# Finishing the softmax sums of a hybrid block's attention on GpSimd

## The chip, the cores and the metric

The kernel runs on one core of a Trainium2 chip. The metric is the device time of one execution in microseconds (us), as the median of several runs. The core has five engines, each with a queue of its own that it works off in order: TensorE (PE, with its weight loads PEld), VectorE (DVE), ScalarE (ACT), GpSimd (POOL) and SyncE (SP), which issues DMAs. ScalarE and GpSimd issue DMAs too, from the same queues as their arithmetic.

## The reference

One layer of a decoder block over 2048 tokens of 1024 features in float32: a combined projection feeds sliding-window attention (8 query heads over 2 key heads of 64, window 128, a learned sink for each head) and a chunkwise mLSTM; both are merged, and a gated feed-forward part follows. The change lies in the softmax of the attention:

```python
m = jnp.maximum(jnp.max(s, axis=-1, keepdims=True), sink)
p = jnp.exp(s - m)
p = p / (jnp.sum(p, axis=-1, keepdims=True) + jnp.exp(sink - m))
o = jnp.einsum('bnhgqk,bnkhd->bnqhgd', p, vb)
```

The sink takes part in the maximum and in the sum, but has no value vector.

## The kernel before

The 2048 tokens go through in four blocks of 512 rows, two blocks to a superblock. The first superblock's attention falls between about 110 and 300 us, the second's between about 760 and 960 us. Float32 products are made of three matmuls of high and low parts; the big projections (`acc` tiles, PSUM) are a long stream of 512-wide matmuls that keeps TensorE going. All matmuls are issued by one helper (L212) and all transposes by another (L217), so the trace shows those two lines; what an operation is, its tiles tell.

The attention is written as `attention(n, ...)`, L957 to L1038, for 128 queries, n = 0 to 15. Because of the window, 128 queries see 128 own keys and the 128 before; the two triangles fit together into one 128x128 tile for each head. The eight heads are treated as two halves of four heads (`jj`):

- Scores: matmuls `mix<-at` (L981 by way of the helper), copied out of PSUM by ScalarE (L985) and merged with the previous keys by VectorE's predicated copy (L987) into `sc[jj]`, a `tm` tile of 128x512.
- Maxima on VectorE (L993 to L996), with the sinks; `es` is the exponent of the sinks (L997, ScalarE).
- For each half four exponentials on ScalarE (L1002), which also add up each row into `sums`.
- For each half: VectorE adds the sinks' share to the sums (L1003), VectorE takes the reciprocal (L1004), GpSimd multiplies the half's 128x512 by it (L1005).
- Some time later (a yield of `L_SOFT` = 8000 on the estimated clock): four transposes a half on TensorE (`mix<-ident,tm`), a copy by ScalarE (L1014) and a masked copy by VectorE (L1018), and the weighted sum of the values (`mix<-tm,at`, L1026).
- The result goes out in a high and a low part: L1030 on ScalarE, L1035 on VectorE, with DMAs from ScalarE's queue (L1032, L1037). The operands of a later n are loaded from the same queue (L954).

GpSimd's queue holds, beside the multiply, the stores of q, k and v (L806, L833, L851, L853), a few operations of the mLSTM (L1098, L1100, and at L1149 a power with exponent -0.5 on 128x4), the power of the norms (L492) and memsets.

Where this work stands among the other is decided twice. Python generators (`spawn`, `tick`) place the attention's pieces in the stream of projection matmuls by a running estimate of TensorE's time; then, after the first block's opening, a scheduler orders each engine's queue by its own simulated timeline (L2237). So an edit in one engine's operations can move the place of operations on all engines. The memsets of constants are at L187 and L188.

Of the kernel before, what the change touches and what calls it, by code (L numbers as in the profile page):

```python
# [10 lines left out]
F32 = mybir.dt.float32  # L11
# [4 lines left out]
ALU = mybir.AluOpType  # L16
# [3 lines left out]
P = 128  # L20
# [53 lines left out]
def decoder_block(ctx: ExitStack, tc: tile.TileContext, a: dict, out: bass.AP, dbg=None):  # L74
# [19 lines left out]
    V, A, T, Q = (InOrder(e) for e in (nc.vector, nc.scalar, nc.tensor, nc.sync))  # L94
    G = nc.gpsimd
# [4 lines left out]
    const = ctx.enter_context(tc.tile_pool(name="const", bufs=1))  # L100
# [13 lines left out]
    def nm(s):  # L114
        uid[0] += 1
        return f"{s}{uid[0]}"
# [68 lines left out]
    halves = const.tile([P, 8], F32, name="halves")  # L185
    nhalf, half_pi = halves[:, 0:4], halves[:, 4:5]
    G.memset(nhalf, -0.5)  # L187
    G.memset(half_pi, PI / 2)  # L188
    inv_freq = const.tile([P, HD // 2], F32, name="inv_freq")
    for i in range(HD // 2):  # L190
# [578 lines left out]
    def superblock(sb):  # L769
# [187 lines left out]
        def attention(n, a_, ahead):  # L957
# [11 lines left out]
            sums = small.tile([P, HQ], F32, tag="sums", name=nm("sums"))  # L969
            es = small.tile([P, HQ], F32, tag="es", name=nm("es"))  # L970
# [27 lines left out]
            for jj in range(2):  # L998
                hs = slice(4 * jj, 4 * jj + 4)
                for i in range(4):  # L1000
                    c = 4 * jj + i
                    A.activation(sc[jj][:, i, :], sc[jj][:, i, :], AF.Exp, bias=nm_[:, c:c + 1], accum_out=sums[:, c:c + 1])  # L1002
                V.tensor_tensor(sums[:, hs], sums[:, hs], es[:, hs], op=ALU.add)  # L1003
                V.reciprocal(sums[:, hs], sums[:, hs])  # L1004
                G.tensor_tensor(sc[jj], sc[jj], sums[:, hs].unsqueeze(2).to_broadcast([P, GQ, P]), op=ALU.mult)  # L1005
            yield L_SOFT
            ps_ = []
# [34 lines left out]
        def attention_stream(u):  # L1042
            a_ = None
            for i in range(u, 2 * NT, 2):
                n = b0 * NT + i
                if a_ is None:
                    while i >= ready[0]:
                        yield 1000.0
                    a_ = load_at(n, nc.sync)
                    yield L_LOAD  # L1050
                    a_ = yield from attention(n, a_, lambda: i + 2 < ready[0])
                else:
                    yield L_LOAD - 1500.0
                    a_ = yield from attention(n, a_, lambda: i + 2 < ready[0])
                done_att[0] += 1
                yield 500.0
# [1179 lines left out]
def build(nc, aps, out):  # L2236
    with tile.TileContext(nc, schedule_with_timeline_sim=True) as tc, ExitStack() as ctx:  # L2237
        decoder_block(ctx, tc, aps, out[0])
# [16 lines left out]
```

## Time and profile before

| quantity | value |
|---|---|
| median of 3 runs | 2663.15 us (2661.76 to 2663.3) |
| the profiled execution | 2668.66 us |
| its span in the profile | 2667.0 us |
| mean granted clock of TensorE | 0.994 |
| exponentials L1002, ScalarE, 128 of them | 0.392 us each |
| GpSimd's multiply L1005, 32 of them | 34.6 us in all |
| GpSimd's stores of q, L806, 32 of them | 17.8 us in all |

The profile is of one execution. Its engines' busy times count arithmetic; a wait is put down to the operation that came last before the waiting instruction began. The granted clock says at what share of its full speed TensorE was allowed to run in a stretch. A row of the timeline gives start and duration in us, the engine, the line, the operation and its tiles, and in brackets the idle time of the engine before it with its releaser; rows that follow each other alike are merged, and the ends of matmuls are modelled.

### The profile page before, as it was taken

What the parts mean: (1) busy time and instruction counts of PE and PEld (TensorE: products, weight loads), DVE (VectorE), ACT (ScalarE), POOL (GpSimd) and SP (SyncE); (2) the same over time, 40 slices, a digit from 0 to 9 for tenths busy, and PEclk for the clock granted to TensorE, in tenths of its full rate; (3) what the DMA queues carried; (4) which work ended last, traced back from release to release, by engine and by line L of the source; (5) the groups of instructions that cost most, each with busy time, mean ns of one, the idle gap of its engine ahead of it and who ended that gap; (6) DMA issues with size and microseconds to landing.
All of it is one profiled execution on the core that took longest, in us unless ns stands there. A gap on an engine that the chain in (4) does not pass through costs nothing.

```text
span 2667.0 us, 36229 instructions
## 1 busy us (share of the span) xinstructions
PE 2615.5 (98%) x12546; PEld 2145.8 (80%) x12546; DVE 1937.2 (73%) x3758; ACT 1281.9 (48%) x2531; POOL 300.3 (11%) x473
## 2 busy tenths in 40 slices
PE   8999999999989999999999999999999999999998
PEld 6877788888876788888878888888778888888876
DVE  5878887768676988875777777775776767676466
ACT  6656544545654654454643433345554333333444
POOL 0320001101132000210001111110000011001000
PEclk9899999999999999999999999999999999999999
DMA  7785465887787545597765554446675323234556
GB/s 270 255 303 164 135 196 183 291 301 253 262 313 244 166 135 181 183 296 268 220 238 193 184 169 153 163 139 228 213 242 173 111 99 116 90 111 139 199 196 220
DMA packets 327032, 532.97 MB, mean 200 GB/s; under 512 B 23136, under 2 KB 197724, under 8 KB 320064
## 3 DMA queue, kind: packets, MB, share of 16 engines
q1 hardware_dynamic: 287752, 448.45, 50.4%
q0 software_dynamic: 20880, 66.41, 6.6%
q10 hardware_dynamic: 18216, 15.79, 1.9%
q8 instruction: 99, 1.62, 0.2%
q14 instruction: 85, 0.70, 0.1%
HBM read 367.61 MB, written 154.57 MB: 196 GB/s over the span
## 4 chain that ended last, share of the span: by engine, by line
PE 88%; DVE 4%; DMA 3%; ACT 2%; issue 1%; POOL 0%; ACTq 0%; SPq 0%; DVEq 0%; POOLq 0%
PE acc L212 62%; PE mix L212 22%; PE mix L217 2%; PE acc L90 1%; DVE hl L1745 1%; PE mix L90 1%; DMA raw<-as_d 1%; ACT hl L1744 1%; DMA big<-big 0%; DMA raw<-ws_d 0%; DMA raw<-in_w_in_dram 0%; ACT tm L1002 0%; DMA at_d<-tx 0%; DMA raw<-in_w_ffn_down_dram 0%; ACT big L575 0%
## 5 line engine op out<-in xcount | busy, mean ns | idle before, releaser
L212 PE MATMUL acc<-big,hl 128*128 128x512 f32 x3936 | 936.4, 393 | 7.0 <-ACT tx L870 5.4
L212 PEld LDWEIGHTS acc<-big,hl 128*128 128x128 f32 x3936 | 733.8, 188 | 166.4 <-ACT tx L870 5.9
L1744 ACT CAST hl<-raw 128x512 fp32r<-128x512 f32 x732 | 439.9, 621 | 489.6 <-PE acc L212 208.7
L1745 DVE TENSOR_TENSOR hl<-raw,hl 128x512 fp32r<-128x512 f32 x732 | 495.1, 692 | 198.4 <-ACT hl L1744 196.0
L212 PE MATMUL acc<-whi,big 128*128 128x512 f32 (+1 forms) x896 | 281.6, 390 | 3.0 <-ACT tx L870 3.0
L212 PE MATMUL mix<-big,hl 128*128 128x512 f32 x1056 | 263.0, 390 | 1.8 <-ACT hl L1744 1.1
L212 PE MATMUL acc<-hl,hl 128*128 128x512 f32 x1008 | 237.2, 393 | 6.2 <-DVE hl L1745 3.3
L212 PEld LDWEIGHTS mix<-big,hl 128*128 128x128 f32 x1056 | 197.8, 188 | 44.5 <-ACT hl L1744 2.0
L212 PEld LDWEIGHTS acc<-hl,hl 128*128 128x128 f32 x1008 | 187.1, 188 | 51.8 <-DVE hl L1745 8.8
L212 PEld LDWEIGHTS acc<-whi,big 128*128 128x128 f32 x896 | 168.6, 192 | 36.2 <-ACT tx L870 3.4
L212 PE MATMUL mix<-hl,hl 128*128 128x512 f32 x792 | 182.7, 391 | 3.4 <-ACT hl L1744 2.6
L212 PEld LDWEIGHTS mix<-hl,hl 128*128 128x128 f32 x792 | 147.8, 188 | 37.6 <-ACT hl L1744 4.2
L212 PE MATMUL acc<-wlo,big 128*128 128x512 f32 (+1 forms) x448 | 174.4, 389 | 0.0
L212 PE MATMUL acc<-big,whi 128*128 128x512 f32 x512 | 157.3, 393 | 0.0
L268 DVE TENSOR_TENSOR wlo<-raw,whi 128x1024 fp32r<-128x1024 f32 (+1 forms) x76 | 90.8, 1194 | 65.7 <-ACT whi L267 60.2
L267 ACT CAST whi<-raw 128x1024 fp32r<-128x1024 f32 (+1 forms) x76 | 78.4, 1032 | 109.7 <-PE acc L212 103.5
L492 POOL TENSOR_TENSOR rs<-ms,halves 128x1 f32<-128x1 f32 (+1 forms) x56 | 41.3, 744 | 797.8 <-DVE ms L490 750.4
L212 PE MATMUL mix<-hcT4h,hl 128*128 128x512 f32 x352 | 115.6, 389 | 0.7 <-ACT hl L1744 0.7
L212 PE MATMUL acc<-hcT2h,hl 128*128 128x512 f32 x352 | 115.5, 389 | 0.0
L212 PEld LDWEIGHTS acc<-big,whi 128*128 128x128 f32 x512 | 95.3, 188 | 19.3
L212 PEld LDWEIGHTS acc<-wlo,big 128*128 128x128 f32 x448 | 85.8, 192 | 18.0 <-issue 1.2
L212 PE MATMUL acc<-big,wlo 128*128 128x512 f32 x256 | 97.6, 392 | 0.0
(388 smaller groups left out, 3802.3 us busy)
## 6 DMA issues: line engine op xcount, KB each, us to landing
as_d<-w POOLq DMA_DIRECT2D x154, 256.0 KB, 2.5
raw<-in_w_in_dram SPq DMA_DIRECT2D x36, 1024.0 KB, 5.4
raw<-as_d SPq DMA_DIRECT2D x70, 512.0 KB, 3.8
raw<-in_w_ffn_gate_dram SPq DMA_DIRECT2D x22, 1024.0 KB, 6.1
raw<-in_w_ffn_up_dram SPq DMA_DIRECT2D x22, 1024.0 KB, 5.8
raw<-ws_d SPq DMA_DIRECT2D x40, 512.0 KB, 4.6
tx<-in_w_ada_dram SPq DMA_DIRECT2D x64, 256.0 KB, 5.3
g_d<-tx SPq DMA_DIRECT2D x64, 256.0 KB, 2.4
```

The source lines that it names most:

```text
L90: self.last = tc.keep_in_program_order(f(*p, **k)).ins
L212: T.matmul(o, lhsT=lhsT, rhs=rhs, start=start, stop=stop, skip_group_check=resumed)
L217: T.transpose(o, i, ident[:k, :k])
L267: A.copy(hv, src)
L268: V.tensor_tensor(lv, src, hv.bitcast(F32), op=ALU.subtract)
L492: G.tensor_tensor(r[:, :n], ms[:, :n], nhalf[:, :n], op=ALU.pow)
L1744: A.copy(v(hi), src)
L1745: V.tensor_tensor(v(lo), src, v(hi).bitcast(F32), op=ALU.subtract)
```

## The change

The add of the sinks' share and the reciprocal move from VectorE to GpSimd, where the multiply already is. GpSimd has the reciprocal as a power with exponent -1, so a constant of four columns of -1 is set up once.

```diff
     G.memset(nhalf, -0.5)
+    minus1 = const.tile([P, 4], F32, name="minus1")
+    G.memset(minus1, -1.0)
     G.memset(half_pi, PI / 2)
...
-                V.tensor_tensor(sums[:, hs], sums[:, hs], es[:, hs], op=ALU.add)
-                V.reciprocal(sums[:, hs], sums[:, hs])
+                G.tensor_tensor(sums[:, hs], sums[:, hs], es[:, hs], op=ALU.add)
+                G.tensor_tensor(sums[:, hs], sums[:, hs], minus1, op=ALU.pow)
                 G.tensor_tensor(sc[jj], sc[jj], sums[:, hs].unsqueeze(2).to_broadcast([P, GQ, P]), op=ALU.mult)
```

All lines behind the new constant are two higher: add L1005, power L1006, multiply L1007, matmul helper L214, transpose helper L219. The set of instructions is otherwise the same: VectorE has 64 fewer, GpSimd 64 more and one memset. The order of the queues around the attention changes, since the scheduler makes it anew. On TensorE, in the first superblock, before, the transposes of n = 6 and 7 stand in a row behind two projection matmuls:

```order
L212 MATMUL acc_3091<-big_565,hl_3027 128x512
L212 MATMUL acc_3091<-big_549,hl_3027 128x512
L217 MATMUL mix_2600<-ident,tm_2433 128x128 x4
L217 MATMUL mix_2619<-ident,tm_2457 128x128 x4
L217 MATMUL mix_2628<-ident,tm_2434 128x128 x4
L217 MATMUL mix_2640<-ident,tm_2458 128x128 x4
```

After, the first half of n = 6 (`tm_2435`) stands four projection matmuls ahead of the next two groups, and the second half of n = 7 is further down:

```order
L219 MATMUL mix_2602<-ident,tm_2435 128x128 x4
L214 MATMUL acc_3093<-big_551,hl_3029 128x512 x2
L214 MATMUL acc_3093<-big_567,hl_3029 128x512
L214 MATMUL acc_3093<-big_551,hl_3029 128x512
L219 MATMUL mix_2621<-ident,tm_2459 128x128 x4
L219 MATMUL mix_2630<-ident,tm_2436 128x128 x4
```

The four groups of transposes no longer stand together: the two halves of n = 6 are apart, and n = 7 has one half with the second of n = 6 and one by itself. The groups on GpSimd and at another place of TensorE are shown in the prediction.

## Prediction

> **What bounds the kernel.** I read the page first: busy time by engine, then the chain that ended last. The first number behind an engine is its busy time, then its share of the span.
>
> ```profile
> PE 2615.5 (98%) x12546; PEld 2145.8 (80%) x12546; DVE 1937.2 (73%) x3758; ACT 1281.9 (48%) x2531; POOL 300.3 (11%) x473
> ...
> PE 88%; DVE 4%; DMA 3%; ACT 2%; issue 1%; POOL 0%; ACTq 0%; SPq 0%; DVEq 0%; POOLq 0%
> ```
>
> TensorE is the bound and is nearly full. An edit of vector work can therefore only act through what TensorE waits for. Next come the waits of PE in the two stretches with attention, 120 to 440 us and 700 to 900 us (total, times, longest):
>
> ```profile
> PE mix L217 <- DVE tm L1035: 1.2, 1, 1.2
> PE acc L212 <- ACT tx L870: 0.8, 1, 0.8
> ...
> PE acc L212 <- ACT tx L870: 4.6, 1, 4.6
> PE acc L212 <- ACT tm L985: 4.2, 1, 4.2
> PE mix L217 <- DVE tm L987: 2.6, 1, 2.6
> PE mix L212 <- ACT tm L1014: 1.7, 2, 1.3
> PE mix L217 <- POOL tm L1005: 0.2, 1, 0.2
> ```
>
> The multiply on GpSimd holds TensorE up once in 32 times, for 0.2 us. The waits of 4.6 and 4.2 us belong to the q/k/v projection and to the copies of scores, ahead of any softmax sum. What the change can reach is the rest: 1.2 + 0.8 + 2.6 + 1.7 + 0.2 = 6.5 us. That is the ceiling of a gain through waits.
>
> Last, the clock that TensorE was granted, in the windows (us from the start; the first column behind the five engines) and the wait ahead of the first of them in the timeline:
>
> ```profile
> 107.80:121.50 13.70, 12.26 (x59) 11.39 (x60) 9.21 (x25) 7.92 (x25) 3.25 (x6) 0.50 0.96 326
> 782.00:786.00 4.00, 1.36 (x12) 1.25 (x11) 3.93 (x16) 1.02 (x5) 1.88 (x4) 1.00 1.04 358
> ```
>
> ```profile
> 108.97 0.59 PE L212 MATMUL acc<-whi,big 128*128 128x264 f32 x1 [2.69 <-ACT tx L870]
> ```
>
> A wait of 2.69 us was followed by 13.7 us at half the clock; the wait of 2.6 us near 784 us was not. A new stall of about that length is thus dearer than its own length.
>
> **The change, part by part.** The durations (ns, min/median/max) and VectorE's idle time ahead of the add:
>
> ```profile
> L1003 DVE TENSOR_TENSOR sums<-sums,es x32: 150/164/766, 120.6 to 940.6; 128x4 f32<-128x4 f32 x32
>   ACT tm L1002: 26.0, 25
> L1004 DVE RECIPROCAL sums<-sums x32: 167/178/179, 120.8 to 940.8; 128x4 f32<-128x4 f32 x32
> L1005 POOL TENSOR_TENSOR tm<-tm,sums x32: 1032/1042/1591, 121.2 to 941.1; 128x512 f32<-128x512 f32 x32
> L1149 POOL TENSOR_TENSOR cf<-vr,halves x16: 1018/1019/1399, 405.9 to 1198.6; 128x4 f32<-128x4 f32 x16
> L187 POOL MEMSET halves<- x1: 103/103/103, 1.0 to 1.0; 128x4 f32 x1
> ```
>
> *Removed from VectorE:* 32 x (0.164 + 0.178) = 10.9 us of work, and 25 places where its queue stood behind an add that waited for the exponentials, 26.0 us. VectorE is 73% busy and not the bound, so this counts only where TensorE waited for it.
>
> *Added to GpSimd, for each half of four heads:* a power on 128x4, which the trace has in the same form at L1149, 1.02 us; and an add on 128x4, which it does not have on this engine. The memset of that size took 0.10 us, the power 1.02 us. These bound the add; since a power is another kind of arithmetic, I take a value near the memset, 0.2 us. [...] The extra memset at the start, 0.1 us, lies under work that the change leaves as it was.
>
> A hand-over between dependent steps takes about 0.17 us: in the next rows (start, duration, engine, line; in brackets the idle time ahead and what ended it) the reciprocal ended at 265.74 and the multiply began at 265.91.
>
> ```profile
> 264.44 0.19 ACT L1002 ACTIVATION_READ_ACCUMULATOR tm<-tm,nmx 128x1 f32 x1
> 269.18 0.19 ACT L1002 ACTIVATION_READ_ACCUMULATOR tm<-tm,nmx 128x1 f32 x1
> 265.56 0.18 DVE L1004 RECIPROCAL sums<-sums 128x4 f32<-128x4 f32 x1
> 265.91 1.04 POOL L1005 TENSOR_TENSOR tm<-tm,sums 128x512 f32<-128x512 f32 x1 [38.82 <-DVE sums L1004]
> 263.70 6.74 PE L212 MATMUL acc<-big,hl 128*128 128x512 f32 x29
> 270.28 1.91 PE L217 MATMUL mix<-ident,tm 128*128 128x128 f32 x16
> ```
>
> So a half now needs 0.2 + 1.02 + 1.04 us on GpSimd and two hand-overs, about 2.6 us. The exponentials of the four halves of n = 6 and 7 end between 264.63 and 269.37, one each (269.37 - 264.63)/3 = 1.58 us: GpSimd is slower than its supply there, and a queue forms. Its order at that place, before (multiplies only; L1149 is later work):
>
> ```order
> L1005 TENSOR_TENSOR tm_2433<-tm_2433,sums_2431 128x512
> L1005 TENSOR_TENSOR tm_2434<-tm_2434,sums_2431 128x512
> L1005 TENSOR_TENSOR tm_2457<-tm_2457,sums_2455 128x512
> L1005 TENSOR_TENSOR tm_2458<-tm_2458,sums_2455 128x512
> L1149 TENSOR_TENSOR cf_4064<-vr_4041,halves 128x4
> ```
>
> and after (lines are 2 higher: L1005 add, L1006 power, L1007 multiply):
>
> ```order
> L1005 TENSOR_TENSOR sums_2433<-sums_2433,es_2434 128x4
> L1006 TENSOR_TENSOR sums_2433<-sums_2433,minus_118 128x4
> L1007 TENSOR_TENSOR tm_2435<-tm_2435,sums_2433 128x512
> L1005 TENSOR_TENSOR sums_2433<-sums_2433,es_2434 128x4
> L1006 TENSOR_TENSOR sums_2433<-sums_2433,minus_118 128x4
> L1005 TENSOR_TENSOR sums_2457<-sums_2457,es_2458 128x4
> L1007 TENSOR_TENSOR tm_2436<-tm_2436,sums_2433 128x512
> L1006 TENSOR_TENSOR sums_2457<-sums_2457,minus_118 128x4
> L1005 TENSOR_TENSOR sums_2457<-sums_2457,es_2458 128x4
> L1007 TENSOR_TENSOR tm_2459<-tm_2459,sums_2457 128x512
> L1006 TENSOR_TENSOR sums_2457<-sums_2457,minus_118 128x4
> L1007 TENSOR_TENSOR tm_2460<-tm_2460,sums_2457 128x512
> ```
>
> Four instructions became twelve. Counted from 264.63 with 0.16 to 0.17 us at each dependent step, the third multiply (n = 7, first half) ends at 272.2 and the fourth at 274.5. On TensorE the scheduler moved the transposes too: n = 6, first half, comes four projection matmuls earlier, the next two halves stay, and n = 7, second half, comes 20 later. One such matmul is 6.74/29 = 0.23 us, so n = 7's first half is asked for at 270.28 - 4 x 0.23 + 0.4 + 4 x 0.23 = 270.7, 1.5 us too early. The scores of n = 7 stand four matmuls earlier in the new order, 0.9 us: **C = +0.7 us** (0 to 1.5).
>
> The new order matters elsewhere as well. **Place A**, TensorE at the end of the first block's projection (180 to 192 us), before: the last transposes of n = 3, nine projection matmuls, then its weighted sum (mix<-tm,at):
>
> ```order
> L217 MATMUL mix_1869<-ident,tm_1736 128x128 x4
> L212 MATMUL acc_1976<-whi_2119,big_768 128x512
> L212 MATMUL acc_1976<-whi_2119,big_767 128x512
> L212 MATMUL acc_1976<-wlo_2120,big_767 128x512
> L212 MATMUL acc_1976<-whi_2119,big_768 128x512
> L212 MATMUL acc_1977<-wlo_2120,big_767 128x512
> L212 MATMUL acc_1977<-whi_2119,big_768 128x512
> L212 MATMUL acc_1977<-whi_2119,big_767 128x512
> L212 MATMUL acc_1977<-wlo_2120,big_767 128x512
> L212 MATMUL acc_1977<-whi_2119,big_768 128x512
> L212 MATMUL mix_1881<-tm_1859,at_1639 64x256 x2
> L217 MATMUL mix_1987<-ident,tx_1920 128x128 x4
> ```
>
> After, in the same place: the weighted sum of n = 2 (mix_1825), the transposes of n = 3 (mix_1856, mix_1871) and its weighted sum (mix_1883) in a row:
>
> ```order
> L214 MATMUL mix_1825<-tm_1803,at_1581 64x256 x2
> L214 MATMUL mix_1825<-tm_1805,at_1581 64x256 x2
> L214 MATMUL mix_1825<-tm_1818,at_1581 64x256 x2
> L219 MATMUL mix_1856<-ident,tm_1737 128x128 x4
> L214 MATMUL mix_1825<-tm_1820,at_1581 64x256 x2
> L219 MATMUL mix_1871<-ident,tm_1738 128x128 x4
> L214 MATMUL mix_1883<-tm_1861,at_1641 64x256 x2
> L219 MATMUL mix_1989<-ident,tx_1922 128x128 x4
> ```
>
> The fourteen projection matmuls that covered the way from transpose over PSUM copy to weighted sum have moved ahead of it. What that way takes bare can be read at 829 us:
>
> ```profile
> 828.58 0.44 PE L217 MATMUL mix<-ident,tm 128*128 128x128 f32 x2
> 829.77 0.59 ACT L1014 COPY tm<-mix 128x512 f32<-128x512 f32 x1 [0.44 <-ACT tm L1030]
> 830.41 0.65 PE L212 MATMUL mix<-tm,at 128*64 128x256 f32 x4 [0.46 <-ACT tm L1014]
> ```
>
> From the end of the transposes, 829.02, to 830.41 is 1.39 us. **A = +1.4 us**: one such way uncovered (0 if the pieces of n = 2 cover it, 2.8 if both halves lie bare). The multiplies are no limit there, since the transposes come later. The same bunching befalls n = 10 and 11 around 828 us, where five projection matmuls (1.1 us) used to lie between: **B = +0.8** (0 to 1.4). For n = 8 (784 us) the first row of the weighted sum now follows its transposes directly, where 18 matmuls lay between; of the 1.39 us the other half's transposes cover 0.4: **D = +1.0** (0 to 1.4).
>
> *Gained* between 776 and 801 us:
>
> ```profile
> 776.78 0.16 DVE L1003 TENSOR_TENSOR sums<-sums,es 128x4 f32<-128x4 f32 x1 [1.32 <-ACT tm L1002]
> 778.32 0.17 DVE L1003 TENSOR_TENSOR sums<-sums,es 128x4 f32<-128x4 f32 x1 [1.17 <-ACT tm L1002]
> 784.15 0.77 DVE L987 COPY_PREDICATED tm<-m_prev,mix 128x256 f32<-128x256 uint32 x2
> 780.40 1.69 PE L212 MATMUL mix<-at 64*128 64x256 f32 x24
> 784.73 1.06 PE L217 MATMUL mix<-ident,tm 128*128 128x128 f32 x8 [2.64 <-DVE tm L987]
> 799.42 0.37 ACTq L1037 DMA_DIRECT2D y_d<-tm  x1
> 800.75 0.65 PE L212 MATMUL mix<-tm,at 128*64 128x256 f32 x4 [1.26 <-ACT tm L1014]
> ```
>
> VectorE stood 1.32 + 1.17 us behind the adds and then had no gap up to L987, for which TensorE waited 2.64 us. With that gone, L987 still has to wait for the scores, which end at 782.09, and for their copies; the multiplies of n = 8, at 2.6 us a half, end near 782. I take **-1.2 us** (0 to -1.6). The 0.2 us at 794 go, as the transposes of n = 9 come 16 matmuls later: **-0.2**. The wait at 800.75 came from a copy queued on ScalarE behind the y DMA of 799.42; in the new order TensorE asks for it 15 matmuls, 3.4 us, later: **-1.3**.
>
> Sum: 1.4 + 0.8 + 0.7 + 1.0 - 1.2 - 0.2 - 1.3 = **+1.2 us**. The profiled run took 2668.66 us, 2667.0 of it span; with the sum it would be 2669.9. Applied to the median of 2663.15 us it gives **2664.4 us**. A measurement of this kernel tells about 0.2% from no change, 5.3 us; the forecast is no measurable change. Its own range, all lower or all upper ends together, is -3.1 to +7.1 us, 2660.1 to 2670.3.
>
> **Rivals.** (1) *Slower: the add costs as much as the power.* Then a half needs 3.45 us, and at C four adds stand ahead of the third multiply: 4 x 0.8 = 3.2 us more. n = 4 and 5 (three halves in one place) and n = 14 and 15 build the same queue, together up to 3.2 again: 2664.4 + 6.4 = 2670.8. For it: the power of the same shape took 1.02 us. Against: the memset's 0.10. It decides from an add of about 0.7 us: eight adds 0.5 us dearer are 4.1, with the 1.2 of the sum 5.3. 0.12.
>
> (2) *Slower: a stall at A or D reaches about 2.7 us and the clock halves.* 13.7 us at half the clock cost 6.9 us: 2671.3. For it: A has 1.2 and 0.8 us of waits already. Against: matmuls lie between those, and 1.4 alone is short. [...] 0.08.
>
> (3) *Slower: small GpSimd work stops VectorE.* Rows at 405 us:
>
> ```profile
> 405.86 1.04 POOL L1149 TENSOR_TENSOR cf<-vr,halves 128x4 f32<-128x4 f32 x1 [134.54 <-DVE vr L1147]
> 406.29 0.68 DVE L1745 TENSOR_TENSOR hl<-raw,hl 128x512 fp32r<-128x512 f32 x1
> 406.88 1.04 POOL L1098 TENSOR_TENSOR tm<-tm,mp 128x512 f32<-128x512 f32 x1
> 406.93 1.01 DVE L1150 TENSOR_TENSOR cf<-cf,den 128x4 f32<-128x4 f32 x1
> ```
>
> VectorE's 128x4 operation beside the 512-wide one took 1.01 us, yet its 128x512 operation that began during the power took an ordinary 0.68. If add and power did block, a half would cost up to 1.2 us of VectorE, and at the four places of the sum 4.9 us: 2669.3. [...] 0.04.
>
> (4) *Faster: the new order covers what I charged for, and VectorE's freed 37 us end the waits.* With A to D at nothing and all 6.5 us of waits gone: 2656.7. It must win 5.3 of 6.5 to be seen. For it: 64 operations and 25 waits leave the second busiest engine. Against: few of those waits stood ahead of TensorE. 0.15.
>
> (5) *Nothing changes*, since PE waits for L1005 0.2 us in all: 2663.2. 0.03, within 0.2% like the forecast, 0.58.
>
> **How the numbers follow.** Faster 0.15; same 0.58 + 0.03 = 0.61; slower 0.12 + 0.08 + 0.04 = 0.24. The range 2657.0 to 2671.0 holds the forecast, the first, third and fifth rival and most of the fourth; the second lies just outside.
>
> **What would show it.** In the changed profile: add near 0.2 us and power near 1.02 on GpSimd; its busy time up by about 32 x 1.22 = 39 us; no idle time of VectorE ahead of those sums; new PE waits of 0.5 to 2 us near 187, 271, 785 and 829 us; none of 2.64 and 1.26. A slower add, a half clock behind one of these places, or a shift above 5.3 us with none of them would prove me wrong.

## The result and the profile after

The changed kernel takes 2688.24 us (median of 4 runs, 2684.68 to 2690.87) against 2662.97 us before: a ratio of 1.0096, 95% interval 1.0084 to 1.0109, or 25 us slower. Forecast were 2664.4 us, and 2671.0 at most. The profiled execution has a span of 2689.2 us, 22.2 us more than that of before.

The page after, busy time by engine and the chain that ended last:

```profile
PE 2631.9 (98%) x12546; PEld 2148.3 (80%) x12546; DVE 1933.9 (72%) x3694; ACT 1281.4 (48%) x2531; POOL 345.3 (13%) x538
...
PE 88%; DMA 4%; DVE 3%; ACT 2%; POOL 1%; issue 1%; SPq 0%; ACTq 0%; POOLq 0%; DVEq 0%
```

TensorE has the same 12546 matmuls and is busy for 16.4 us more. So waits can be only a part of the loss; the larger part is matmuls that took longer. To see where, I take the k-th projection matmul (`acc`) of both traces as a mark and compare the stretches between the marks:

| stretch (matmul of projection, counted) | before, us | after, us | difference |
|---|---|---|---|
| start to 80 | 51.0 | 53.4 | +2.4 |
| 80 to 300 | 48.9 | 49.3 | +0.4 |
| 300 to 600, attention n = 0 to 3 | 96.4 | 98.8 | +2.4 |
| 600 to 1000, n = 4 to 7 | 112.9 | 113.7 | +0.8 |
| 1000 to 2800 | 446.9 | 446.8 | -0.1 |
| 2800 to 3040, n = 8 to 11 | 79.4 | 83.1 | +3.7 |
| 3040 to 3480, n = 12 to 15 | 133.1 | 137.1 | +4.0 |
| 3480 to 5040 | 399.5 | 399.3 | -0.2 |
| 5040 to the end, mostly feed-forward | 1298.9 | 1307.6 | +8.7 |

The attention, of which alone the prediction speaks, has 10.9 of 22 us. The opening and the feed-forward part, where no instruction was changed, have 11.5. In the feed-forward part one family of matmuls is slower throughout, those that stream an `hcT` tile, as the groups of TensorE show (busy us, mean ns); before:

```profile
L212 PE MATMUL mix<-hcT4h,hl 128*128 128x512 f32 x352 | 115.6, 389 | 0.7 <-ACT hl L1744 0.7
L212 PE MATMUL acc<-hcT2h,hl 128*128 128x512 f32 x352 | 115.5, 389 | 0.0
L212 PE MATMUL mix<-hcT4l,hl 128*128 128x512 f32 x176 | 68.5, 389 | 0.0
L212 PE MATMUL acc<-hcT2l,hl 128*128 128x512 f32 x176 | 68.5, 389 | 0.0
```

and after:

```profile
L214 PE MATMUL mix<-hcT4h,hl 128*128 128x512 f32 x352 | 117.9, 396 | 0.7 <-ACT hl L1746 0.7
L214 PE MATMUL acc<-hcT2h,hl 128*128 128x512 f32 x352 | 117.8, 395 | 0.0
L214 PE MATMUL mix<-hcT4l,hl 128*128 128x512 f32 x176 | 69.6, 396 | 0.0
L214 PE MATMUL acc<-hcT2l,hl 128*128 128x512 f32 x176 | 69.6, 395 | 0.0
```

Each is 6 to 7 ns longer, and from start to start they come every 0.232 to 0.235 us (medians of the groups) instead of 0.227. (The busy time of a group is less than count times mean, since matmuls overlap.) The two largest groups, `acc<-big,hl` and `acc<-hl,hl`, keep 0.227 us. Over the two stretches in which they stand, without waits, TensorE needs 4.1 + 4.1 us more: 7.1 of it in these four groups, 1.0 in the `mix<-big,hl` matmuls between them.

On GpSimd the three operations of a half (ns, min/median/max):

```profile
L1005 POOL TENSOR_TENSOR sums<-sums,es x32: 189/200/1498, 122.5 to 950.2; 128x4 f32<-128x4 f32 x32
L1006 POOL TENSOR_TENSOR sums<-sums,minus x32: 1001/1008/1863, 122.8 to 951.8; 128x4 f32<-128x4 f32 x32
L1007 POOL TENSOR_TENSOR tm<-tm,sums x32: 1039/1041/1562, 123.9 to 953.3; 128x512 f32<-128x512 f32 x32
```

The three prices are the ones that the prediction took: 0.2, 1.0 and 1.04 us. From the last exponential to the end of the multiply, a first half takes 2.6 us (median; 1.75 before) and a second one 4.1 (1.95 before). The waits of TensorE (total, times, longest), from 120 to 440 us and, since the second attention now ends later, from 700 to 1000 us; before, no wait is added between 900 and 1000 us:

```profile
PE mix L214 <- DVE tm L1020: 1.9, 1, 1.9
PE mix L219 <- POOL tm L1007: 1.5, 2, 1.0
PE acc L214 <- ACT tx L872: 0.9, 1, 0.9
...
PE mix L219 <- POOL tm L1007: 2.3, 2, 2.2
PE mix L219 <- DVE tm L989: 2.0, 1, 2.0
PE mix L214 <- ACT tm L1016: 1.2, 1, 1.2
PE mix L214 <- DVE tm L989: 0.8, 1, 0.8
```

The multiply now holds TensorE up four times, for 3.8 us instead of 0.2. Two of these are at place A, in the timeline:

```profile
185.17 1.08 PE L214 MATMUL mix<-tm,at 128*64 128x256 f32 x8 [1.92 <-DVE tm L1020]
186.84 1.11 PE L219 MATMUL mix<-ident,tm 128*128 128x128 f32 x4 [0.58 <-POOL tm L1007]
187.88 1.12 PE L214 MATMUL mix<-tm,at 128*64 128x256 f32 x4
189.97 1.11 PE L219 MATMUL mix<-ident,tm 128*128 128x128 f32 x4 [0.97 <-POOL tm L1007]
```

Four transposes take 1.11 us there; at the same place before they took 0.60 to 0.66. The windows say why (the clock is the first column behind the five engines):

```profile
183.00:186.40 3.40, 1.34 (x12) 0.49 (x8) 3.40 (x7) 3.28 (x13) 2.93 (x3) 1.00 0.00 0
186.40:193.20 6.80, 5.40 (x22) 2.83 (x24) 3.60 (x5) 1.75 (x3) 3.36 (x4) 0.50 0.26 77
787.00:790.50 3.50, 1.52 (x26) 1.35 (x23) 3.46 (x9) 1.96 (x8) 3.48 (x6) 1.00 1.09 352
790.50:797.40 6.90, 6.10 (x20) 4.30 (x20) 6.73 (x29) 4.53 (x8) 1.30 (x3) 0.51 0.45 172
```

At A and near 790 us TensorE was busy for about 40% of some 3.4 us, and then ran 6.8 us at half the clock. The wait inside the first window is the 1.92 us of the timeline, that inside the third is one of 1.98 us for L989.

### The profile page after: what moved, and what is told of

Its sections match the earlier page's. It is cut to its first block, busy times and chain, and to the rows that moved or that the text cites. A ratio compares the mean times of both kernels' runs of the same rounds, so it can differ in the third digit from the quotient of the medians.

```text
span 2689.2 us, 36225 instructions
## 1 busy us (share of the span) xinstructions
PE 2631.9 (98%) x12546; PEld 2148.3 (80%) x12546; DVE 1933.9 (72%) x3694; ACT 1281.4 (48%) x2531; POOL 345.3 (13%) x538
## 4 chain that ended last, share of the span: by engine, by line
PE 88%; DMA 4%; DVE 3%; ACT 2%; POOL 1%; issue 1%; SPq 0%; ACTq 0%; POOLq 0%; DVEq 0%
PE acc L214 62%; PE mix L214 22%; PE mix L219 2%; PE acc L90 1%; DMA raw<-in_w_ffn_down_dram 1%; DVE hl L1747 1%; PE mix L90 1%; ACT hl L1746 1%; DMA raw<-w_kv_d 0%; DMA raw<-ws_d 0%; DMA big<-big 0%; DMA raw<-in_w_in_dram 0%; ACT tm L1004 0%; DMA big<-in_x_dram 0%; DMA raw<-as_d 0%
## 5 line engine op out<-in xcount | busy, mean ns | idle before, releaser
L214 PE MATMUL acc<-big,hl 128*128 128x512 f32 x3936 | 939.0, 393 | 6.5 <-ACT tx L872 4.8
L214 PEld LDWEIGHTS acc<-big,hl 128*128 128x128 f32 x3936 | 733.9, 188 | 167.3 <-issue 6.3
L214 PE MATMUL acc<-whi,big 128*128 128x512 f32 (+1 forms) x896 | 278.3, 386 | 1.7 <-ACT tx L872 1.7
L214 PE MATMUL mix<-big,hl 128*128 128x512 f32 x1056 | 264.1, 391 | 2.0 <-ACT hl L1746 1.4
L214 PE MATMUL acc<-hl,hl 128*128 128x512 f32 x1008 | 237.4, 393 | 5.9 <-DVE hl L1747 3.5
L214 PEld LDWEIGHTS mix<-big,hl 128*128 128x128 f32 x1056 | 197.8, 188 | 46.5 <-ACT hl L1746 2.2
L214 PEld LDWEIGHTS acc<-hl,hl 128*128 128x128 f32 x1008 | 186.9, 188 | 51.8 <-DVE hl L1747 9.1
L214 PEld LDWEIGHTS acc<-whi,big 128*128 128x128 f32 x896 | 166.6, 189 | 34.6 <-ACT tx L872 1.8
L214 PE MATMUL mix<-hl,hl 128*128 128x512 f32 x792 | 182.9, 391 | 3.7 <-ACT hl L1746 2.8
L214 PEld LDWEIGHTS mix<-hl,hl 128*128 128x128 f32 x792 | 147.7, 188 | 38.2 <-ACT hl L1746 4.2
L214 PE MATMUL acc<-wlo,big 128*128 128x512 f32 (+1 forms) x448 | 172.9, 387 | 0.0
L214 PE MATMUL acc<-big,whi 128*128 128x512 f32 x512 | 157.3, 392 | 0.0
L214 PE MATMUL mix<-hcT4h,hl 128*128 128x512 f32 x352 | 117.9, 396 | 0.7 <-ACT hl L1746 0.7
L214 PE MATMUL acc<-hcT2h,hl 128*128 128x512 f32 x352 | 117.8, 395 | 0.0
L214 PEld LDWEIGHTS acc<-big,whi 128*128 128x128 f32 x512 | 95.3, 188 | 19.3
L1966 POOL DMA_DIRECT2D as_d<-w x66 | 35.8, 542 | 517.2 <-DVE w L1961 517.2
L214 PEld LDWEIGHTS acc<-wlo,big 128*128 128x128 f32 x448 | 84.9, 189 | 16.6 <-DVE wlo L270 0.3
```

Of the source, the lines that this page charges most:

```text
L214: T.matmul(o, lhsT=lhsT, rhs=rhs, start=start, stop=stop, skip_group_check=resumed)
L1966: G.dma_start(as_d[b2][:, IDX[names[qd]], p, :], g[qd])
```

## The experiments

Two theories stood at the start. **L**, layout: the new constant takes 32 bytes in each partition (16 of them data) and moves every tile behind it by as much; the `hcT` tiles, which are placed from the upper end of the memory, stay. That slows matmuls and loads that have nothing to do with the change. **Q**, GpSimd's path: a multiply that ends later holds TensorE up, at a rate that grows with the path. Their rivals were G (everything comes from GpSimd and the order, nothing from the layout), O (the scheduler's closer order does the damage, whatever the length of the path) and D (VectorE's relief gives part of it back).

**1. The constant alone** (`e1_pad`).

```diff
 (kernel before)
     G.memset(nhalf, -0.5)
+    minus1 = const.tile([P, 4], F32, name="minus1")
+    G.memset(minus1, -1.0)
```

> The kernel before, with the new constant of four columns and its memset, and nothing that uses it: every queue is in the order of before, and every tile allocated behind the constant lies 32 bytes higher in each partition. Theory L (layout): the feed-forward matmuls whose moving operand is an hc tile (fixed at the upper end of the memory) and whose stationary operand is an hl tile (moved by 32 bytes) start every 0.235 us instead of 0.227 us, 1056 of them, about +8.3 us: near 2671.3 us, with the attention stages as before. Rival G (all of the loss comes from GpSimd and the order): 2663 us, no change.

2675.88 us against 2661.96, ratio 1.0052 (1.0035 to 1.0069): 14 us, for a tile that nobody reads. The `hcT` matmuls take 396 and 395 ns as in the changed kernel, 8.1 us in the two stretches. The attention stages from 600 to 3480 are within 0.3 us of those of before. That of n = 0 to 3 is 2.9 us shorter, with all queues in the order of before: its profile has 3.4 us at half the clock there instead of 13.7. `pad64` and `pad128` below, again in the order of before, have 6.8 and 0 us, so the order alone does not settle how long the half clock lasts behind the same waits. L had forecast 8.3 us; it had not forecast the 2.6 us that the stretch up to the 80th projection matmul lost. What is slow there is the loads; windows of 5 to 45 us in before, `e1_pad`, the changed kernel and the next run (last two columns: DMA share, GB/s):

```profile
5.00:45.00 40.00, 36.30 (x225) 25.65 (x225) 22.70 (x62) 23.33 (x37) 1.45 (x2) 1.00 1.06 381
5.00:45.00 40.00, 36.72 (x229) 25.57 (x233) 22.62 (x62) 21.74 (x34) 1.44 (x2) 1.00 1.08 358
5.00:45.00 40.00, 36.19 (x225) 25.62 (x225) 22.71 (x62) 21.80 (x35) 1.45 (x2) 1.00 1.08 359
5.00:45.00 40.00, 36.50 (x223) 25.99 (x224) 22.68 (x62) 23.91 (x38) 1.45 (x2) 1.00 1.05 380
```

The queues are full in all four (a DMA share of 1.05 to 1.08), and with moved tiles they carry 6% less, 358 and 359 GB/s instead of 381 and 380. Who waits for it can be seen on ScalarE, before and after:

```profile
43.95 1.06 ACT L90 ACTIVATE big<-big 128x1024 f32<-128x1024 f32 x1 [0.92 <-DMA big<-in_x_dram]
```

```profile
46.40 1.06 ACT L90 ACTIVATE big<-big 128x1024 f32<-128x1024 f32 x1 [3.29 <-DMA big<-in_x_dram]
```

The same first norm of rows starts 2.45 us later because a block of x lands later.

**2. The change without the shift** (`e2_addr`).

```diff
 (changed kernel)
-    negc = const.tile([P, 1], F32, name="negc")
+    negs = const.tile([P, 8], F32, name="negc")
+    negc, minus1 = negs[:, 0:1], negs[:, 1:5]
...
-    minus1 = const.tile([P, 4], F32, name="minus1")
```

> The changed kernel with its constant put into the unused columns of an existing tile, so that every tile lies where it lay before the change; instructions and their order are those of the changed kernel. Theory L: the hc matmuls go back to 0.227 us, 8.3 us are won, near 2680 us, and what is left over the kernel before, about 17 us, is attention, clock and the opening. Rival G: 2688 us.

2675.07 us, ratio 1.0046 (1.0031 to 1.0062), +13 us. The `hcT` matmuls are back at 389 ns, the opening at 380 GB/s and within 0.4 us of before up to the 80th projection matmul. Shift alone 14 and the rest alone 13 make 27; the change measures 25. L holds, and more is in it than it said; G falls.

**3. Both operands shifted** (`e3_both`).

```diff
 (changed kernel)
-        hcp.tile([P, 248], F32, name="hc_end")
+        hcp.tile([P, 240], F32, name="hc_end")
```

> The changed kernel, with the constant where the change puts it, and the hc tiles moved up by 32 bytes as well (a filler tile beside them made 32 bytes smaller). If what counts is how the two operands lie to each other (modulo 64 bytes), the hc matmuls go back to 0.227 us: near 2680 us. If what counts is that hl no longer lies on a multiple of 64 bytes, they stay at 0.235 us: 2688 us. Rival G: 2688 us.

2678.60 us, ratio 1.0065 (1.0048 to 1.0083). The four groups read 115.6, 115.5, 68.5 and 68.5 us at 389 ns, as before. So for these matmuls it is how the streamed tile lies to the stationary one that counts (389 ns with both moved, 395 to 396 with one), not either address by itself. The opening stays at 359 GB/s: for its loads it is the address itself.

**4. How coarse the grid is** (`pad64`, `pad128`): as in 1, with 16 and with 32 columns.

```diff
-    minus1 = const.tile([P, 4], F32, name="minus1")
+    minus1 = const.tile([P, 16], F32, name="minus1")
```

> The kernel before with an unused constant of 16 columns, 64 bytes, so that all tiles behind it lie 64 bytes higher; every queue is in the order of before. Theory L64 (what counts is the address modulo 64 bytes): hc matmuls at 0.227 us, about 380 GB/s in the opening, 2662 us. Rival (any shift of the tiles against the hc tiles, or any new constant, does it): 2675 us as with 32 bytes.

> The kernel before with an unused constant of 32 columns, 128 bytes, so that all tiles behind it lie 128 bytes higher; every queue is in the order of before. Theory L128 (what counts is the address modulo 128 bytes): hc matmuls at 0.227 us, about 380 GB/s in the opening, 2662 us. Rival L512 (a coarser grid: in the kernel before, the big tiles, the split tiles and the hc tiles all lie on multiples of 512 bytes): 0.233 us or more, about 359 GB/s, 2675 us.

2674.77 us (ratio 1.0044, 1.0029 to 1.0059) and 2676.25 us (1.0058, 1.0041 to 1.0075): both as slow as 32 bytes. The `hcT` matmuls take 394 to 395 ns, the opening runs at 359 GB/s in both. L64 and L128 fall. In the kernel before, the split tiles, the big tiles and the `hcT` tiles all begin at multiples of 512 bytes; the grid is thus coarser than 128.

Whether it is 256 or 512 can be read from the raw tiles. One of their buffers takes 8 x 264 x 4 = 8448 bytes, so of the two the second begins 256 bytes past a multiple of 512. Matmuls that stream 512 columns of a raw tile against a big tile follow each other every 0.227 us (medians) from either buffer, in the kernel before and in `e1_pad`, where all these tiles are moved. The packet records of the opening's loads say the same. Packets of 1024 bytes, most of them into big tiles, take 46 ns (median) in the kernel before and 51 with tiles 32, 64 or 128 bytes off the grid. Packets of 2048 bytes into raw tiles take 84 ns before, into the second buffer as into the first, and 87 to 90 with moved tiles. A shift by 256 bytes thus cost neither these matmuls (0.227 us) nor these loads (84 ns) anything here, while one by 128 cost both (394 to 395 ns for an `hcT` matmul instead of 389, 359 GB/s instead of 381).

**5. The reciprocal alone, and the add alone** (`e4_pow`, `e5_add`), both in the layout of before.

```diff
 (e4_pow, e2_addr as base)
-                G.tensor_tensor(sums[:, hs], sums[:, hs], es[:, hs], op=ALU.add)
+                V.tensor_tensor(sums[:, hs], sums[:, hs], es[:, hs], op=ALU.add)
 (e5_add, kernel before as base)
-                V.tensor_tensor(sums[:, hs], sums[:, hs], es[:, hs], op=ALU.add)
+                G.tensor_tensor(sums[:, hs], sums[:, hs], es[:, hs], op=ALU.add)
```

> Layout of before; the add stays on VectorE, only the reciprocal goes to GpSimd as a power. A half needs 2.2 us on GpSimd instead of 2.6. Theory Q (a queue forms on GpSimd because a half needs longer than the 1.58 us in which the next one comes): still a queue, waits of TensorE for the multiply of 3 to 8 us instead of 12, near 2673 us. Rival O (the length counts little, the scheduler's closer order does the damage): as much as the whole change in the layout of before, near 2680 us.

> Only the add goes to GpSimd (0.2 us), the reciprocal stays on VectorE, the layout is that of before. A multiply ends some 0.3 us later than before through the extra hand-over. Theory Q (loss grows with the time from exponentials to multiply): 0 to 3 us, near 2664 us. Rival O (a new order of TensorE and freed waits of VectorE decide, whatever the length): anything up to the whole change's 13 us.

2668.01 us, ratio 1.0024 (1.0014 to 1.0034), and 2662.87 us against 2662.90, ratio 1.0009 (1.0000 to 1.0019). The power costs 6 us, the add alone nothing to speak of. Q had put `e4_pow` at 2673 by way of waits for the multiply of 3 to 8 us; TensorE waits for it nowhere in that run, and its weight loads 0.8 us, so the 6 us do not come the way that Q said. The multiplies end 2.9 and 3.4 us behind the exponentials. Against `e1_pad`, the profile is 3.6 us longer in n = 0 to 7 and 1.7 in n = 8 to 15, but the clock alone moves a stretch by nearly as much (2.9 us for n = 0 to 3 in experiment 1); where the 6 us arise is not shown.

**6. The path lengthened** (`pow3`).

```diff
 (e2_addr as base)
                 G.tensor_tensor(sums[:, hs], sums[:, hs], minus1, op=ALU.pow)
+                G.tensor_tensor(sums[:, hs], sums[:, hs], minus1, op=ALU.pow)
+                G.tensor_tensor(sums[:, hs], sums[:, hs], minus1, op=ALU.pow)
```

> The changed kernel in the layout of before, with the power with exponent -1 done three times in a row, which gives the same reciprocal: two more powers of 1.01 us and two hand-overs, about 2.2 us more for each half on GpSimd, 4.7 us instead of 2.5. Theory Q: the loss grows steeply, since two halves now come every 3.1 us and need 9.4: 2690 to 2705 us. Rival O: as the changed kernel in this layout, 2675 us within 5.

2697.98 us, ratio 1.0136 (1.0119 to 1.0153), +35 us, as Q had it. The row of TensorE's waits for the multiply, 3.7 us in `e2_addr`, is now the largest:

```profile
PE mix L219 <- POOL tm L1009: 22.3, 12, 5.9
```

**7. The same order on TensorE, two paths** (`p0_pinned`, `p1_pinned_gpsimd`).

```diff
 (p0: kernel before; p1: e2_addr)
-            if not pinned[0]:
+            if not pinned[0] and self.eng is not nc.tensor:
                 return f
```

> The kernel before with TensorE kept in the order in which the program was written (the scheduler orders only the other engines). It is the partner of the next run, and its own time is not forecast: the order is another one, 2665 to 2690 us.

> Add and power on GpSimd in the layout of before, with TensorE kept in program order as in its partner: TensorE's queue is the same in both, instruction by instruction. Theory Q (what costs is that the multiplies end later, 2.5 and 3.9 us behind the exponentials instead of 1.6 and 2.0): slower than the partner by 3 to 10 us. Rival O (what costs is the scheduler's new, closer order of TensorE): the partner's time within 2 us.

2866.85 us (2861.81 to 2871.11) and 2876.62 us (2873.37 to 2884.39). TensorE's order is a much worse one, but the same in both, and GpSimd's longer path costs 10 us in it. The waits for the multiply, first p0, then p1:

```profile
PE mix L90 <- POOL tm L1005: 19.8, 9, 4.0
```

```profile
PE mix L90 <- POOL tm L1007: 28.0, 16, 4.3
```

That is 8.2 us more of waiting for the multiply. The rows do not add up to the 10 us: other waits became shorter, and the two profiled executions are only 2.8 us apart, with 10 us less at half the clock in p1's. But every one of the four times of p1 lies above every one of p0's. So O is not needed for a loss of this size; without any new order the path alone makes one. It does not follow that the order adds nothing in the scheduled kernel.

**8. VectorE keeps its work** (`dve_kept`).

```diff
 (e2_addr as base)
-    small.tile([P, 8], F32, name="small_end", bufs=1)
+    unused = small.tile([P, 8], F32, name="small_end", bufs=1)
...
+                V.tensor_tensor(unused[:, hs], sums[:, hs], es[:, hs], op=ALU.add)
+                V.reciprocal(unused[:, hs], unused[:, hs])
                 G.tensor_tensor(sums[:, hs], sums[:, hs], es[:, hs], op=ALU.add)
```

> The changed kernel in the layout of before, and VectorE does its add and its reciprocal as well, into a tile that nobody reads: VectorE keeps the work and the waits that the change takes from it, GpSimd's path is that of the change. Theory Q (the loss comes from GpSimd's path, VectorE's relief is worth little): 2675 us within 3, as without them. Rival D (VectorE's relief hides a part of the loss): 2680 us or more.

2673.44 us, ratio 1.0046 (1.0031 to 1.0061), against 2675.07 without. With the 64 operations and their waits back on VectorE the kernel is not slower, and D, which asked for 2680 us or more, falls. It is no clean pair: the scheduler ordered TensorE anew, and 6% of the places in its queue hold another operation than in `e2_addr`.

**9. Two attempts to win something back** (`l11_later`, `mp_merged_gpsimd`) **and one to improve on before** (`mv_merged_dve`).

```diff
 (l11, e2_addr as base)
-L_SOFT, L_PT, L_PV = 8000.0, 1300.0, 1000.0
+L_SOFT, L_PT, L_PV = 11000.0, 1300.0, 1000.0
 (mp, e2_addr as base: one add and one power on 128x8 behind both halves' exponentials;
 the two lines inside the loop are gone, and the multiplies stand in a loop of their own)
+            G.tensor_tensor(sums, sums, es, op=ALU.add)
+            G.tensor_tensor(sums.rearrange("p (j i) -> p j i", j=2), sums.rearrange("p (j i) -> p j i", j=2), minus1.unsqueeze(1).to_broadcast([P, 2, 4]), op=ALU.pow)
 (mv, kernel before as base: the same on VectorE)
+            V.tensor_tensor(sums, sums, es, op=ALU.add)
+            V.reciprocal(sums, sums)
...
```

> The changed kernel in the layout of before, with the wait written between softmax and transposes raised from 8000 to 11000, so that transposes are asked for about 3 us later. Theory Q: TensorE's waits for the multiply (3.7 us, and 8.1 us at weight loads) go, and the half clock behind them: near 2666 us. Rival O: the order stays as close as it is, near 2675 us.

> The changed kernel in the layout of before, with one add and one power on 128x8 for both halves behind the last exponential, then the two multiplies: GpSimd needs about 3.5 us for 128 queries instead of 5.2, and the second half's multiply ends about 3.5 us behind its exponentials instead of 3.9, the first half's 4.0 instead of 2.5. Theory Q: the queue at n = 6 and 7 and at n = 14 and 15 goes, single halves wait a little longer: near 2670 us. Rival O: 2675 us or any other time that the new order makes.

> The kernel before with one add and one reciprocal on 128x8 for both halves on VectorE behind the last exponential: VectorE has 32 operations fewer and waits once instead of twice, the first half's multiply ends 3.1 us behind its exponentials instead of 1.6, the second's 2.6 instead of 2.0. Theory Q: slower, by 3 to 8 us, 2665 to 2670 us. Rival D (VectorE's freed operations and waits are what counts): faster, 2655 to 2660 us.

`l11_later`: 2676.78 us, ratio 1.0054 (1.0039 to 1.0069), no gain; TensorE waits 5.0 us for the multiply, more than the 3.7 in its base. A later place in the program only moved the rest of the chain too, and Q's forecast of 2666 was wrong. `mp_merged_gpsimd`: 2684.18 us, ratio 1.0083 (1.0068 to 1.0098), worse: less work for GpSimd, but both halves end later, 4.9 and 4.6 us behind their exponentials. `mv_merged_dve`: 2665.95 us, ratio 1.0014 (1.0004 to 1.0023), 3 us slower with 32 operations fewer on VectorE.

The runs in the layout of before, in order of the time from a half's last exponential to the end of its multiply (medians over 16 first and 16 second halves), against the kernel before as measured together with each. The last column is the share of places in TensorE's queue that hold another operation than in the kernel before, counted on the programs as built:

| kernel | first, second half, us | slower by, us | TensorE's order changed |
|---|---|---|---|
| before | 1.75, 1.95 | 0 | 0 |
| `e5_add` | 1.7, 1.8 | 0 | 2% |
| `mv_merged_dve` | 3.2, 2.8 | 3 | 5% |
| `e4_pow` | 2.9, 3.4 | 6 | 4% |
| `e2_addr` (the change) | 2.6, 4.0 | 13 | 9% |
| `dve_kept` | 2.7, 4.0 | 12 | 7% |
| `l11_later` | 2.6, 4.1 | 15 | 10% |
| `mp_merged_gpsimd` | 4.9, 4.6 | 22 | 10% |
| `pow3` | 6.5, 11.3 | 35 | 12% |

The loss grows with the path and not with the number of VectorE's operations. But TensorE's order moves away from that of before along with it, so the table does not tell the path from the order that the scheduler makes of it. None of these beats the kernel before.

## Why the prediction was wrong, point by point

**The step that failed first: what the change touches.** The part-by-part list priced a memset of 0.1 us for the constant and called the opening unchanged work. The constant's 32 bytes were in the diff, and they cost 14 of the 25 us: some 8.1 us in the stretches of the `hcT` matmuls, 2.4 to 2.6 us in the loads of the opening, and a rest that the stretches of one profile do not show apart. The source had a hint: L101, L103 and L1756 allocate tiles (`const_end`, `small_end`, `hc_end`) that no operation touches, and that only move what is placed behind them. Eight columns fewer in `const_end` would have left all tiles behind the constant in place (not run). No rival named it; none could, since all were built on the engines' queues.

**The step that failed next: a wait was priced at its own length.** The other 13 us come from the moved work and its new order. The sum counts waits alone, and half the clock was left to a rival at 0.08. From the 300th to the 3480th projection matmul, the four profiles in the order of before (before, `e1_pad`, `pad64`, `pad128`) have TensorE idle for 18.8 to 21.3 us and at half the clock for 10 to 21 us. The three in the changed order (the changed kernel, `e2_addr`, `e3_both`) have 21.1 to 23.4 us idle and 27 to 34 us at half the clock, 6.8 us each time at A and near 790 us. By the means, the stretch is 11.3 us longer: 2.6 us are idle time, and 12.6 us more of matmul work at half the clock make an estimated 5.9 us, since 512-wide matmuls begin every 0.427 us there instead of 0.227 (medians, before and after). By this estimate the slow clock behind the waits cost more than the waits.

**GpSimd's prices were right.** Add 0.200 us, power 1.008, multiply 1.041. The hand-overs are shorter than taken, 0.08 us, as these rows for n = 6 show:

```profile
268.86 0.20 POOL L1005 TENSOR_TENSOR sums<-sums,es 128x4 f32<-128x4 f32 x1 [34.06 <-ACT tm L1004]
269.14 1.02 POOL L1006 TENSOR_TENSOR sums<-sums,minus 128x4 f32<-128x4 f32 x1
270.24 1.04 POOL L1007 TENSOR_TENSOR tm<-tm,sums 128x512 f32<-128x512 f32 x1
```

**C, +0.7 us: nothing.** TensorE does not wait at n = 6 and 7. The first half of n = 7 is multiplied by 275.80 and asked for at 277.17. The queue on GpSimd formed as worked out, but the transposes come later against the exponentials than the prediction had them.

**A, +1.4 us: too small, and the wrong limit.** The prediction let one way from transposes to weighted sum lie bare and said that the multiplies were no limit. They were: TensorE waits 0.58 and 0.97 us for the two halves of n = 3, after 1.92 us for the masked copy ahead of the weighted sum of n = 2, and 0.88 at the end; 4.35 us of waits where there had been 2.04. The wait of 1.92 us also brought the half clock that the prediction had kept for a rival. That the multiply became a limit here is more than the longer path. Before, the multiplies of n = 3 ended 3.2 and 2.7 us ahead of their transposes, and the path grew by 1.9 and 2.9 us. In the new order the scores of n = 3 also end behind the 557th projection matmul instead of the 530th, about 6 us later.

**D, +1.0, and the gain of -1.2.** Both came about in kind. The wait of 2.64 us is now 1.98, a gain of 0.7, and a new one of 0.80 follows:

```profile
790.34 1.76 PE L219 MATMUL mix<-ident,tm 128*128 128x128 f32 x8 [1.98 <-DVE tm L989]
792.89 1.12 PE L214 MATMUL mix<-tm,at 128*64 128x256 f32 x4 [0.80 <-DVE tm L989]
```

What was not foreseen is that the shorter wait is followed by 6.8 us at half the clock, where the longer one had been followed by none. That alone costs an estimated 2.8 us: TensorE is busy for 6.0 of these 6.8 us, and 512-wide matmuls begin every 0.427 us at half the clock instead of 0.227. Rival 2 below says why.

**B, +0.8:** a wait of 1.2 us on L1016 at 840 us, where the same place had 0.46 before: +0.74. **The gains of -0.2 and -1.3** at 794 and 800 us came true. The upper end of the prediction's own range, +7.1, leaves these two gains out; with them it is +5.6, and the measured time lies outside either way.

**n = 12 to 15, taken at nothing: +4.0 us.** The prediction summed up four places and left the last four n alone. But before, the multiplies of n = 15 ended only 0.86 and 0.16 us ahead of their transposes, and the first of n = 13 1.0 us. At 951.9 us TensorE now stands 2.15 us for n = 15:

```profile
951.90 1.09 PE L219 MATMUL mix<-ident,tm 128*128 128x128 f32 x8 [2.15 <-POOL tm L1007]
```

Here it is the path: the first multiply of n = 15 ended 1.6 us behind its exponentials before and 4.7 us after. Of the 4.0 us an estimated 0.6 are chance: near 860 us both kernels fall to half the clock, for 3.4 us before and 6.8 after, with TensorE busy for 3.4 and 4.6 us of it, and `pad64` and `pad128`, in the order of before, have 6.8 there as well. In `e2_addr` the stretch is only 1.3 us longer than before.

**Rival 1** had the right mechanism at n = 14 and 15, a queue on GpSimd that TensorE waits for, but the wrong condition: it needed no dear add. **Rival 2** had the right effect and the wrong condition. It asked for a stall of 2.7 us; waits of 1.9 and 2.0 us were enough. In the traces the clock changes in steps of 3.41 us, and a half clock goes with how little of the step ahead of it TensorE was busy. Counted in those steps from the first clock record, in 16 profiles, no step at full clock with under 42% busy was followed by another at full clock, and none with over 68% by one at half; between the two, both happen. The wait of 2.64 us before lay across a border (782.09 to 784.73, border near 783.6) and left TensorE busy for over half of each step, 1.86 and 2.32 of 3.41 us:

```profile
780.23:783.64 3.41, 1.86 (x26) 1.51 (x25) 3.34 (x17) 1.76 (x8) 3.10 (x6) 1.00 1.08 352
783.64:787.05 3.41, 2.32 (x15) 2.08 (x16) 3.41 (x15) 1.82 (x4) 0.55 (x1) 1.00 1.01 390
```

The 1.98 us after lay within one step. The prediction went by the length of a single pause. In its example, the 13.7 us at half the clock began at 107.82 us, inside the wait of 2.69 us (106.28 to 108.97), at the end of a step with TensorE busy for 1.56 of 3.41 us.

**Rival 3**, small GpSimd work that stops VectorE, has no run of its own. VectorE was busy for 1937.2 us before and 1933.4 in `e2_addr`, with 13.6 us of operations taken from it, so its others took some 10 us longer; 64 more powers, 72 us of GpSimd's time, add only 4 us to that (`pow3`, 1937.3). Whether any of it reaches TensorE is not shown. **Rival 4**, VectorE's freed 37 us, shows no worth: with them taken back (`dve_kept`) the kernel is not slower. **Rival 5**, no change, falls with the 25 us.

**What stays open.** `e4_pow` is 6 us slower with hardly a wait for the multiply, so the longer path also works through the order that the scheduler makes of it, or through later work of the same n. Experiment 7 shows that the path alone can cost 10 us, in another order; in the scheduled kernel n = 15 points to the path and n = 3 in part to the order, and how the 13 us divide between them is open. Of these 13 us the rows of `e2_addr` give about 11: compared with `e1_pad`, n = 0 to 3 are 5.1 us longer, 4 to 7 1.9, 8 to 11 3.0, 12 to 15 1.4. By the same two profiles an estimated 7 of the 11 are half clock.

## What to carry to other kernels

Before pricing the instructions of an edit, look at what it allocates: a small constant ahead of large tiles moves them all, and in this kernel, whose tiles lie on a grid, that cost as much as the work that was moved (14 us and 13). Put such a constant into unused columns of an existing tile, and test a change that adds one against the same allocation without its use. For a path that ends just in time in front of the bound engine, count its length from producer to consumer for every place at which it has no slack; relief on an engine that nobody waits for does not pay for it (the time was 2673 us with VectorE's work taken back, 2675 without). Price a new wait with the clock behind it: here the matmuls at half the clock cost an estimated 5.9 us, the added idle time 2.6. And where a scheduler makes the order anew, compare with a pinned order before blaming the instructions.

## What the runs showed of the hardware

- Loads: in the opening, with the DMA queues full, big and raw tiles were filled at 379 to 381 GB/s with big tiles on 512-byte multiples (nine kernels), at 358 to 359 with all of them 32, 64 or 128 bytes further (five kernels). A raw buffer 256 bytes past such a multiple was as fast as one on it, 84 ns for a packet of 2048 bytes. With the tiles 32, 64 or 128 bytes further, such a packet took 87 to 90 ns.
- TensorE: with a 512-column float32 operand streamed from a tile whose address differs from the stationary tile's grid by 32, 64 or 128 bytes, matmuls began every 0.231 to 0.237 us (medians); with both on the grid, both 32 bytes off it, or one 256 bytes from the other's grid, every 0.227.
- Clock: in steps of 3.41 us, TensorE's full clock fell to half behind every step with under 42% busy and behind none with over 68% (16 profiles). In four kernels with the same order of TensorE, the half clock behind the waits near 108 us lasted 0, 3.4, 6.8 and 13.7 us.
- GpSimd: an add on 128x4 took 0.20 us, a power on the same shape 1.01, a multiply on 128x512 1.04. So on 128x4 the power took five times as long as the add.
